# A QKV projection on one core: the first load of x issued as two transfers of one row tile each

## The chip, the cores and the metric

The kernel runs on one core of a Trainium2 chip. Its engines run their own instruction streams side by side: TensorE (PE; its weight loads are listed as PEld), VectorE (DVE), ScalarE (ACT), GpSimd (POOL) and SyncE (SP), which here only issues DMA transfers. Sixteen DMA engines move the bytes. The metric is the device time of one execution in microseconds (us); lower is better.

## The reference

x has 16 x 512 rows of 768 numbers, 8192 rows in all, and w_qkv is 768 x 2304. One product gives q, k and v, which are stacked:

```python
def reference(x, w_qkv):
    qkv = np.matmul(x, w_qkv)
    hidden = x.shape[-1]
    q = qkv[..., :hidden]
    k = qkv[..., hidden:2*hidden]
    v = qkv[..., 2*hidden:]
    return np.stack([q, k, v], axis=0).astype(np.float32)
```

## The kernel before, in words

The 8192 rows are worked on as 32 pairs of row tiles; a row tile has P = 128 rows, and a pair is 256 rows x 768 numbers, 768 KB in fp32. The contraction of K = 768 is cut into KT = 6 slices of 128. Of the 2304 output columns, 2048 are cut into four blocks of 512, which belong to two halves q = 0 and 1, and 256 remain (`rem`). From pair 2 on, a pair and a half q are multiplied by a scheme with seven products in place of eight (`product`, L247), on sums of blocks of x and w that VectorE and GpSimd make ahead. The first two pairs are done by plain bf16 products (`block`, L480), because the sums of w are not there yet.

The order of the work on each engine is the order in which the program writes it (`manual_schedule`, L57). Waits are put in by the tile framework: an instruction waits for whatever wrote the part of a tile that it reads. DMA transfers on SP's queue take eight semaphores in turn, and a transfer is issued only once the transfer eight before it on that rotation has landed.

What happens at the start, in the order in which it is written:

- L452: VectorE clears the tile `zero`.
- L453: `load_rows(0)` loads pair 0 in row order into `xin`, a tile of 128 x 2 x 768: partition m holds row m of both row tiles. It is one transfer of 768 KB (L162).
- L456: `load_rows(1)` does the same for pair 1.
- L457 to L463: the loads of the weights: the first block of 512 columns in six transfers of 256 KB (`load_blocks(0, 0, 1)`), the second in two of 768 KB, the remaining columns (`st_rem`), pair 2 of x in eight pieces (L460, L462), and so on. All go through SP's queue.
- L538: ten matmuls on `zero` on TensorE (`busy(10)`, L469), whose results nobody reads.
- L539: `cast_rows(0)` rounds pair 0 to bf16 row tile by row tile: for each r, VectorE takes the first 384 numbers of each row (L165) and ScalarE the others (L166).
- L540: `turn_rows(0)` transposes pair 0 on TensorE, six transposes for each row tile (L185); VectorE (L194) and ScalarE (L192) copy the results to `xb`. `cast_rows(1)` stands between the two engines' copies.
- L541 to L546: two more matmuls on `zero`, the casts of the first weights' slices (L476), then `turn_rows(1)`, and the casts of the other slices.
- L547: `block(0, 0, ...)`: the first real matmuls (L496), by slices of the weights as these come in: slices 0 and 1 for the two row tiles of pair 0, then the same for pair 1, then slices 2 to 5 for all four row tiles.

From there to the end TensorE has a long stream of matmuls (L258, L321, L496).

Of the kernel before, what the change touches and what calls it, by code (L numbers as in the profile page):

```python
# [10 lines left out]
def kernel(  # L11
# [20 lines left out]
    nc = tc.nc  # L32
    P = 128
# [20 lines left out]
    x_flat = x.rearrange("b t h -> (b t) h")  # L54
# [66 lines left out]
    xin, xf, xb, sr = {}, {}, {}, {}  # L121
# [34 lines left out]

    def load_rows(p):
        xin[p] = xin_pool.tile([P, 2, K], fp32, name="xin")  # L160
        rows = x_flat[p * 2 * P:(p + 1) * 2 * P, :]
        nc.sync.dma_start(xin[p][:], rows.rearrange("(r m) k -> m r k", m=P))  # L162

    def copy_halves(dst, src):
        nc.vector.tensor_copy(out=dst[0], in_=src[0])  # L165
# [284 lines left out]
    ND = 2  # L450
    zero = xb_pool.tile([P, CB], bf16, name="zero", tag="xb")
    nc.vector.memset(zero[:], 0.0)  # L452
    load_rows(0)  # L453
    nc.scalar.activation(tiny[:], zero[:, :1], ident)
    make_identity(nc, eye)
    load_rows(1)  # L456
    load_blocks(0, 0, 1)  # L457
    load_blocks(0, 1)
# [246 lines left out]
```

## Time and profile before

| | |
|---|---|
| median of 3 runs | 359.29 us (359.18 to 359.3) |
| the profiled execution's own time | 358.81 us |
| its span, first to last instruction | 357.0 us |
| TensorE busy | 350.6 us (98%) |
| VectorE, ScalarE, GpSimd busy | 264.4, 185.0, 177.3 us |
| moved by DMA | 108.10 MB, 303 GB/s over the span |
| first load of x issued, and read by the casts | 0.74 us, 4.97 us |
| second load of x issued, and read by the casts | 1.24 us, 6.93 us |
| first matmul of the first block | 8.29 us |

Busy time counts an engine's working instructions. Times in the timeline are microseconds from the first instruction of the span; a matmul's end is modelled, so that the end of one and the start of the next can overlap. In the chain of work that ended last, every link is what the next one waited for.

### The profile page before, as it was taken

Reading aid. Unit: us, or ns where it says so; the run is one execution under the profiler, and the core shown is the slowest. Engines: PE = TensorE matmul, PEld = TensorE weight load, DVE = VectorE, ACT = ScalarE, POOL = GpSimd, SP = SyncE. Lnnn points to the kernel's source line nnn. Section 1 sums busy time; section 2 is a strip of 40 time slices with the busy share of each in tenths; the row PEclk is TensorE's granted clock in tenths of the full one; section 3 lists DMA queues with packets and bytes.
Section 4 is the critical chain, followed back from the end, with each engine's and each line's share of the span. In section 5 each row is a group of like instructions: output and inputs, shape, how many; then the busy total and the mean of one; then the engine's idle time right before and its main releaser. Section 6 shows DMA issues by size and latency. Waiting matters only on the chain.

```text
span 357.0 us, 5315 instructions
## 1 busy us (share of the span) xinstructions
PE 350.6 (98%) x1757; PEld 252.1 (71%) x1776; DVE 264.4 (74%) x310; ACT 185.0 (52%) x317; POOL 177.3 (50%) x184
## 2 busy tenths in 40 slices
PE   7999999999999999999999999999999999999996
PEld 3474677768677686877768677686877768677674
DVE  3789876796877869777695877869777695876743
ACT  4587754545454553645545454553645545454553
POOL 0031773376566453665535566353665535566320
PEclk9999999999999999999999999999999999999999
DMA  7997999999999898998979899698999979887497
GB/s 296 380 353 238 325 378 340 373 317 348 308 311 340 257 361 206 347 266 285 361 197 385 227 342 307 209 402 213 347 263 307 331 196 392 225 303 280 155 380 260
DMA packets 82075, 108.10 MB, mean 303 GB/s; under 512 B 4992, under 2 KB 62080, under 8 KB 82048
## 3 DMA queue, kind: packets, MB, share of 16 engines
q1 hardware_dynamic: 75088, 102.52, 85.7%
q10 hardware_dynamic: 6960, 5.24, 5.5%
q8 instruction: 14, 0.23, 0.3%
q14 instruction: 13, 0.11, 0.1%
HBM read 32.24 MB, written 75.50 MB: 302 GB/s over the span
## 4 chain that ended last, share of the span: by engine, by line
PE 74%; POOL 15%; DVE 6%; issue 3%; DMA 2%; ACT 0%; SPq 0%
PE ps L258 56%; PE ps L321 12%; PE ps L496 6%; DVE xf L155 6%; POOL xb L205 5%; POOL s L226 3%; POOL s L225 3%; POOL s L227 3%; DMA xin<-in_x_dram 2%; PE ps L185 0%; DVE o L304 0%; ACT xc L166 0%; SPq L162 0%; DVE orem L424 0%; ACT orem L423 0%
## 5 line engine op out<-in xcount | busy, mean ns | idle before, releaser
L258 PE MATMUL ps<-t,s 128*128 128x512 f32 x720 | 177.9, 395 | 0.0
L258 PEld LDWEIGHTS ps<-t,s 128*128 128x128 f32 x720 | 135.1, 188 | 29.5
L155 DVE STREAM_TRANSPOSE xf<-xin 128x768 f32<-128x768 f32 (+1 forms) x45 | 93.3, 2075 | 4.3 <-DMA xin<-in_x_dram 4.3
L258 PE MATMUL ps<-b,xb 128*128 128x512 bf16 x343 | 81.6, 379 | 1.1
L298 DVE TENSOR_TENSOR o<-o,ps 128x512 f32<-128x512 f32 x56 | 38.5, 688 | 50.7 <-ACT o L297 50.0
L205 POOL CAST xb<-xf 128x1536 bf16<-128x1536 f32 x28 | 41.1, 1467 | 56.9 <-DVE xf L155 54.8
L225 POOL TENSOR_TENSOR s<-xf 128x384 fp32r<-128x384 f32 x29 | 31.0, 1068 | 72.9 <-DVE xf L155 71.1
L258 PEld LDWEIGHTS <-xb 128*128 128x128 bf16 x360 | 33.9, 98 | 36.7 <-issue 3.9
L304 DVE TENSOR_TENSOR o<-o,ps 128x512 f32<-128x512 f32 x60 | 41.1, 687 | 20.5 <-PE ps L258 19.4
L297 ACT ACTIVATE o<-ps 128x512 f32<-128x512 f32 x56 | 33.5, 598 | 42.1 <-PE ps L258 42.1
L258 PE MATMUL ps<-b,s 128*128 128x512 f32 x180 | 50.6, 389 | 0.0
L301 ACT ACTIVATE o<-ps 128x512 f32<-128x512 f32 x60 | 35.9, 598 | 25.2 <-PE ps L258 22.8
L378 DVE TENSOR_TENSOR o<-o,ps 128x512 f32<-128x512 f32 x78 | 47.8, 680 | 0.0
L321 PE MATMUL ps<-w_rem,xb 128*128 128x256 bf16 x384 | 47.4, 273 | 0.0
L286 ACT ACTIVATE o<-ps 128x512 f32<-128x512 f32 x60 | 35.9, 599 | 19.4 <-PE ps L258 14.0
L321 PEld LDWEIGHTS <-xb 128*128 128x128 bf16 x384 | 37.3, 98 | 11.5 <-issue 0.5
L335 ACT ACTIVATE orem<-ps 128x512 f32<-128x512 f32 x31 | 18.5, 598 | 48.3 <-PE ps L321 34.0
L258 PEld LDWEIGHTS ps<-b,s 128*128 128x128 f32 x180 | 33.8, 188 | 7.0
L226 POOL TENSOR_TENSOR s<-s,xf 128x384 fp32r<-128x384 f32 x29 | 29.5, 1018 | 2.3
L227 POOL TENSOR_TENSOR s<-xf 128x384 fp32r<-128x384 f32 x29 | 29.4, 1015 | 0.0
L229 POOL TENSOR_TENSOR s<-xf,s 128x384 fp32r<-128x384 f32 x29 | 29.2, 1008 | 0.0
L382 ACT ACTIVATE o<-ps 128x512 f32<-128x512 f32 x26 | 15.5, 598 | 17.9 <-PE ps L258 17.3
(49 smaller groups left out, 161.2 us busy)
## 6 DMA issues: line engine op xcount, KB each, us to landing
out_dram<-o SPq DMA_DIRECT2D x60, 768.0 KB, 4.6
out_dram<-o SPq DMA_DIRECT2D x75, 256.0 KB, 3.8
xin<-in_x_dram SPq DMA_DIRECT2D x88, 192.0 KB, 5.6
out_dram<-orem SPq DMA_DIRECT2D x31, 256.0 KB, 2.2
xin<-in_x_dram ACTq DMA_DIRECT2D x24, 192.0 KB, 4.4
st<-in_w_qkv_dram SPq DMA_DIRECT2D x5, 768.0 KB, 7.9
xin<-in_x_dram SPq DMA_DIRECT2D x2, 768.0 KB, 4.9
st<-in_w_qkv_dram SPq DMA_DIRECT2D x6, 256.0 KB, 6.0
```

The lines of the kernel that those rows point to most:

```text
L155: nc.vector.transpose(turned[:, g:g + n], rows[:, g:g + n])
L205: nc.gpsimd.tensor_copy(out=xb[p][:], in_=xf[p][:])
L225: 1: lambda g: g.tensor_tensor(s[:, 1], a21, a22, op=add),
L226: 2: lambda g: g.tensor_tensor(s[:, 2], s[:, 1], a11, op=sub),
L227: 3: lambda g: g.tensor_tensor(s[:, 3], a11, a21, op=sub),
L258: nc.tensor.matmul(ps[:], lhs[j], rhs[j], start=(start and j == 0), stop=(j == KH - 1), skip_group_check=True,)
L286: nc.scalar.activation(c12, u.x[:], ident)
L298: nc.vector.tensor_tensor(c22, c22, u.y[:], op=add)
L301: nc.scalar.activation(c21, u.x[:], ident)
L304: nc.vector.tensor_tensor(c12, c12, u.y[:], op=add)
L321: nc.tensor.matmul(ps, xb[p][:, j, r * P:(r + 1) * P], w_rem[j // KH][:, j % KH, :], start=(j == 0), stop=(j == KT - 1), skip_group_check= ...
L378: dve.tensor_tensor(c, c, u.z[:], op=add)
```

## The change

`load_rows` gets a second argument, a list of parts, each a slice of the partitions and of the row tiles, and issues one transfer per part. Its default is the whole tile as one transfer, so that `load_rows(1)` is what it was. The first call gives two parts: all 128 partitions of row tile 0, then all 128 partitions of row tile 1. In place of one transfer of 128 x 2 x 768 numbers there are two of 128 x 768, one behind the other on SP's queue, into the same tile. Each cast of row tile 0 then waits for the first of them alone, and each cast of row tile 1 for the second. Line numbers below L162 grow by one.

```diff
-    def load_rows(p):
+    def load_rows(p, parts=((slice(0, P), slice(0, 2)), )):
         xin[p] = xin_pool.tile([P, 2, K], fp32, name="xin")
-        rows = x_flat[p * 2 * P:(p + 1) * 2 * P, :]
-        nc.sync.dma_start(xin[p][:], rows.rearrange("(r m) k -> m r k", m=P))
+        rows = x_flat[p * 2 * P:(p + 1) * 2 * P, :].rearrange("(r m) k -> m r k", m=P)
+        for m, r in parts:
+            nc.sync.dma_start(xin[p][m, r], rows[m, r])
...
-    load_rows(0)
+    load_rows(0, [(slice(0, P), r) for r in range(2)])
     nc.scalar.activation(tiny[:], zero[:, :1], ident)
     make_identity(nc, eye)
     load_rows(1)
```

## The prediction

> **What bounds the kernel now.** I read the page's first two parts, then the chain that ended last at the start of the kernel, then the timeline of that stretch, then the DMA rate in half-microsecond windows. The page first: engine totals and the share of the chain by engine.
>
> ```profile
> PE 350.6 (98%) x1757; PEld 252.1 (71%) x1776; DVE 264.4 (74%) x310; ACT 185.0 (52%) x317; POOL 177.3 (50%) x184
> ...
> PE 74%; POOL 15%; DVE 6%; issue 3%; DMA 2%; ACT 0%; SPq 0%
> ```
>
> TensorE works 350.6 of 357.0 us. The change touches only the first load, so it can move the end only if it moves when TensorE's unbroken stream begins. The chain (start, length, what) says what sets that:
>
> ```profile
> 0.74 0.44 SPq L162
> 1.18 0.06 issue
> 1.24 5.67 DMA xin<-in_x_dram
> 6.91 0.02 issue
> 6.93 0.53 ACT xc L166
> ...
> 7.51 0.95 PE ps L185 x12
> 8.46 2.82 PE ps L496 x13
> ...
> 11.33 7.50 PE ps L496 x34
> ```
>
> The link that ends last is the second load of x (issued at 1.24, landed at 6.91), not the first. Behind it come ScalarE's cast of pair 1, its transposes and, from 8.46, matmuls without a gap worth naming. The timeline of the same stretch (start, length, engine, line, operation, idle before):
>
> ```profile
> 0.74 0.95 SPq L162 DMA_DIRECT2D xin<-in_x_dram  x2
> ...
> 1.19 4.30 PE L469 MATMUL ps<-zero 128*128 128x512 bf16 x10 [1.19 <-DVE zero L452]
> ...
> 4.97 0.94 ACT L166 ACTIVATE xc<-xin 128x384 bf16<-128x384 f32 x2 [2.74 <-DMA xin<-in_x_dram]
> 4.97 0.63 DVE L165 CAST xc<-xin 128x384 bf16<-128x384 f32 x2 [3.84 <-DMA xin<-in_x_dram]
> ...
> 6.12 0.77 DVE L194 COPY xb<-ps 128x384 bf16<-128x384 bf16 x2 [0.52 <-PE ps L185]
> ...
> 6.93 0.94 ACT L166 ACTIVATE xc<-xin 128x384 bf16<-128x384 f32 x2 [1.02 <-DMA xin<-in_x_dram]
> ...
> 7.51 0.95 PE L185 MATMUL ps<-eye,xc 128*128 128x128 bf16 x12 [0.58 <-ACT xc L166]
> ...
> 8.26 0.43 DVE L476 CAST b<-st 128x512 bf16<-128x512 f32 x1 [0.27 <-DMA st<-in_w_qkv_dram]
> ...
> 10.85 0.43 DVE L476 CAST b<-st 128x512 bf16<-128x512 f32 x1 [0.28 <-DMA st<-in_w_qkv_dram]
> ```
>
> The casts of pair 0 wait for the first load until 4.97. TensorE is in its ten filler matmuls until 5.49 all the same, and it later stands still for 0.58 us because pair 1 is late. The windows (stretch, busy time of the engines, clock, DMA share, GB/s):
>
> ```profile
> 1.50:2.00 0.50, 0.50 (x2) 0.15 (x1) 0.00 (x0) 0.50 (x1) 0.00 (x0) 1.00 0.57 86
> 2.00:2.50 0.50, 0.50 (x3) 0.21 (x2) 0.00 (x0) 0.22 (x2) 0.00 (x0) 1.00 0.46 92
> 2.50:3.00 0.50, 0.50 (x3) 0.23 (x2) 0.00 (x0) 0.00 (x0) 0.00 (x0) 1.00 0.80 264
> 3.00:3.50 0.50, 0.50 (x3) 0.17 (x2) 0.00 (x0) 0.00 (x0) 0.00 (x0) 1.00 1.01 412
> ```
>
> The transfers start slowly and from 3.0 us run at some 410 GB/s. So the landing at 6.91 is bytes at full rate behind a slow start.
>
> **The change, part by part.** Nothing is removed from the work: the same 768 KB go to the same tile, as two transfers of 384 KB in place of one.
>
> *The rows land apart.* Load 0 is usable at 4.97 and load 1, of the same size, at 6.93: 1.96 us for 768 KB when queued, 0.98 for half. So row 0 should be usable near 4.97 - 0.98 = 3.99, and row 1 at 4.97 as before. Row 0's casts (ScalarE 0.47, VectorE 0.32 us) move from 4.97 to 3.99; row 1's start at 4.97 in place of 5.3 to 5.4. ScalarE then ends pair 0 near 5.50 in place of 5.91.
>
> *What that is worth to TensorE.* The transposes of pair 0 stand behind the ten fillers (1.19 + 4.30 = 5.49) and began at 5.55: 0.06 us to gain. The twelve took 0.95 us with a wait for ScalarE's second cast among them, so perhaps 0.2 us more. Both are given back at once: next in TensorE's order are two fillers and then pair 1's transposes, which need load 1's landing. The idle 0.58 us grows to about 0.8. On the path: 0. Next late is load 1, as now. VectorE, which ended its copies at 6.89 and so was free only just before 6.93, gets some 0.2 us of air; it gains nothing either.
>
> *One more issue on SP.* The two issues of L162 take 0.95 us, some 0.5 each, so everything behind is issued 0.5 us later: load 1 at 1.75 in place of 1.24, the six pieces of the weights' first block each 0.5 later. What hides it: the DMA engines have load 0's bytes to move until nearly 4.97, three microseconds past the later issue, and the pieces find load 1's 1.96 us ahead of them. Were that cover gone, the cost would be the 0.5 us, 359.8.
>
> *One wait more.* Transfers on SP's queue take turns on eight semaphores, and each waits for the one eight before. With one more at the head, the sixth piece of the weights becomes the ninth transfer and waits for row 0's landing; before, it waited for nothing. That wait ends near 4.0, and the piece could not be issued before 4.37 (its issue in SP's own rows) + 0.5 = 4.87 anyway: nothing. Behind it stands the first three-slice load of the second block; it waits for row 1 at 4.97 as it waited for load 0 at 4.97, is issued some 0.4 us later, and has over 4 us of queued bytes in front. All transfers after that wait for the same predecessors as before, and no instruction of TensorE or GpSimd changes.
>
> *The cost of a transfer of its own.* The trace has no split load. Bounds come from the nearest rows: VectorE's waits for pieces at 8.26 and 10.85 are four pieces of 256 KB apart, 0.65 us each or 405 GB/s; the 768 KB load took 1.96, or 401 GB/s. Three small pieces cost as much as one large transfer (1.94 against 1.96), so a queued transfer's own cost is 0 within some 0.03 us. That is the lower end. The upper end is the very first load: 0.74 to 4.97 is 4.23 us, 2.27 above the 1.96. I take 0.02, since row 1 is queued like the pieces and not first in an empty queue. A gain is not excluded: the slow start costs (412 GB/s x 1.16 us - 221 KB) / 412 = 0.62 us by the windows from the first bytes near 1.84 to 3.0, and a shorter first transfer might start otherwise.
>
> The Trainium skill, page "DMA: Bandwidth & Descriptors", section "Rules for kernel authors", speaks against the change: it wants 1 MiB or more per transfer for full bandwidth and small ones merged. The trace does not bear it out between 256 and 768 KB (405 against 401 GB/s), which is why the rival below built on it is small.
>
> The sum: load 1 lands 0.02 us later and all of TensorE's stream with it. The profiled execution has span 357.0 and 1.81 us around it, 358.81; with 0.02 it is 358.83. The median of the runs, 359.29, is 0.48 above that execution, so I put 0.02 on the median: 359.31, in round numbers 359.3.
>
> **The rivals.**
> - *The head of the queue runs better.* The slow start shrinks, and load 1 and the pieces land sooner. For it: 0.62 us lies there, and VectorE is now free in time to use it. Against: total bytes and issue time of the first transfer stay. TensorE's own order bounds it: 0.58 idle + 0.06 + 0.2 = 0.84 us, 358.45.
> - *The slow start comes again at row 1.* Price 0.62 us, at most the whole 1.16 us of 1.84 to 3.0: 359.9 to 360.45. For it: each engine's first packets were slow. Against: load 1, queued too, moved at full rate from its start (412 GB/s in the window from 3.0, 406 in that from 4.0 to 5.0).
> - *A transfer's fixed cost is paid by each.* This is the other side: row 1 or load 1 starts only when what is before it has landed. Price 2.27 us, 361.6; it decides from 0.72 us, a third of it. Against: the row at 6.93 came 1.96 us after that at 4.97, with no such cost. The skill's page named above has a fixed cost of some 2.0 us in its fit for the GpSimd path (section "Anatomy of one DMA — SWDGE (gpsimd) path"); by that the time would be 361.3.
> - *TensorE's clock falls in the longer gap.* The fillers ran at 0.43 us each until about 5 us, later matmuls at 0.217 (2.82 / 13). Were the 0.8 us idle enough to lose the full rate, another 4 us at half would cost some 2 us: 361.3. Against: the 0.58 us gap now did not lose it, as the 0.217 after it shows.
> - *The change doesn't do what it says*: the casts wait for both transfers. Then row 0's casts stay at 4.97 and the time is the forecast's, since nothing follows from them.
>
> **How the numbers follow.** About 0.2% (0.72 us) is what a measurement of this kernel can tell from no change. Nothing moves (with or without early casts): 0.50, 359.0 to 359.6. Better head: 0.20, of which 0.11 beyond 0.2%, where it fills the whole gap. Slow start again: 0.14, half of it beyond. Fixed cost: 0.08. Clock: 0.05. Other causes: 0.03, two thirds of it faster. So faster 0.13, slower 0.07 + 0.08 + 0.05 + 0.01 = 0.21, same 0.66. The range takes in the better head and the slow start but for its last tenth or so, and leaves out the fixed cost and the clock: 358.4 to 360.3.
>
> **What would show it.** Right: in the timeline of the changed kernel VectorE's and ScalarE's first casts stand alone near 4.0 and the second ones at 4.97; pair 0's transposes start near 5.5; pair 1's casts stay at 6.93, the idle before its transposes is near 0.8, and L496 follows at 8.46. The prediction is wrong if the casts of pair 1 move by more than 0.3 us, if TensorE's matmuls after the gap run at 0.43, or if L496 begins later though pair 1's casts do not, which would be the weights' pieces (their 0.5 us later issue) showing.

## The result, and the profile after

The change makes the kernel slower: 361.54 us median (360.51 to 363.76) against 359.26 (359.09 to 359.4), a ratio of 1.0073 with a 95% interval of 1.0048 to 1.0097. The forecast was 359.3, the range 358.4 to 360.3. The profiled execution took 360.70 us with a span of 358.9, 1.9 us more than before's 357.0. The kernel before repeats itself to 0.3 us; the changed one is spread over 3 us, and the profiled execution is one of its fastest, 0.84 us below the median.

First the two lines of the changed kernel's page that answer to those of before: engine totals, and the chain that ended last by engine.

```profile
PE 351.7 (98%) x1776; PEld 252.2 (70%) x1776; DVE 264.1 (74%) x310; ACT 185.4 (52%) x317; POOL 177.3 (49%) x184
...
PE 93%; DMA 4%; SPq 1%; DVE 1%; ACT 0%; issue 0%; DVEq 0%
```

TensorE works as long as before, within what missing records allow; 1.9 us have come in as waiting. The timeline of the changed kernel's start (start, length, engine, line, operation, idle before) shows where:

```profile
3.60 0.52 ACT L167 ACTIVATE xc<-xin 128x384 bf16<-128x384 f32 x1 [1.37 <-DMA xin<-in_x_dram]
...
5.62 0.52 ACT L167 ACTIVATE xc<-xin 128x384 bf16<-128x384 f32 x1 [1.50 <-DMA xin<-in_x_dram]
...
8.16 0.94 ACT L167 ACTIVATE xc<-xin 128x384 bf16<-128x384 f32 x2 [2.02 <-DMA xin<-in_x_dram]
8.74 0.95 PE L186 MATMUL ps<-eye,xc 128*128 128x128 bf16 x12 [1.57 <-ACT xc L167]
...
9.53 5.34 PE L497 MATMUL ps<-b,xb 128*128 128x512 bf16 x24
...
19.23 0.56 DVE L560 CAST w_rem<-str 128x768 bf16<-128x768 f32 x1 [0.83 <-DMA str<-in_w_qkv_dram]
...
20.61 3.04 DVE L155 STREAM_TRANSPOSE xf<-xin 128x768 f32<-128x768 f32 x2 [0.82 <-DMA xin<-in_x_dram]
...
23.13 1.47 PE L259 MATMUL ps<-b,xb 128*128 128x512 bf16 x6
...
24.44 1.47 PE L322 MATMUL ps<-w_rem,xb 128*128 128x256 bf16 x12
```

Row 0 is read 1.37 us earlier than the whole load was (3.60 against 4.97). But load 1, which nothing in the change touches, is read at 8.16 in place of 6.93, TensorE stands idle 1.57 us in place of 0.58, and the first block starts at 9.53 in place of 8.29: +1.24. The other 0.6 us have come in by 24.44, the answer to before's 22.58 (+1.86): the remaining columns of w are cast at 19.23 in place of 17.28, and VectorE's transposes of pair 2 start at 20.61 in place of 18.62, because these loads are late too. The same places in the kernel before:

```profile
17.28 0.56 DVE L559 CAST w_rem<-str 128x768 bf16<-128x768 f32 x1
...
18.62 3.17 DVE L155 STREAM_TRANSPOSE xf<-xin 128x768 f32<-128x768 f32 x2 [0.78 <-DMA xin<-in_x_dram]
...
22.58 1.47 PE L321 MATMUL ps<-w_rem,xb 128*128 128x256 bf16 x12
```

The chain of the changed kernel (start, length, what) goes through that wait, no longer through load 1:

```profile
2.64 6.82 DMA st<-in_w_qkv_dram
...
9.48 0.66 SPq L92
...
10.18 1.77 SPq L137
...
12.64 7.86 DMA xin<-in_x_dram
...
20.61 1.60 DVE xf L155
...
22.23 0.85 ACT xb L215
...
23.13 1.47 PE ps L259 x6
```

It shows transfers waiting for landings and pair 2's x behind them. The windows of the changed kernel (stretch, busy times, clock, DMA share, GB/s) show what the DMA engines do while load 1 should arrive:

```profile
2.00:2.50 0.50, 0.50 (x3) 0.21 (x2) 0.00 (x0) 0.22 (x2) 0.00 (x0) 1.00 1.03 399
...
3.50:4.00 0.50, 0.50 (x2) 0.15 (x1) 0.36 (x1) 0.41 (x1) 0.00 (x0) 1.00 0.92 295
4.00:5.00 1.00, 1.00 (x5) 0.40 (x4) 0.00 (x0) 0.12 (x1) 0.00 (x0) 1.00 0.90 203
5.00:5.50 0.50, 0.47 (x7) 0.33 (x5) 0.00 (x0) 0.00 (x0) 0.00 (x0) 1.00 0.78 264
```

The start is better than before's in this trace (399 GB/s at 2.0 to 2.5, before 92). The loss comes after it: 203 GB/s at a busy share of 0.90, so the engines are counted busy with few bytes. The packet records say the same: in the kernel before no packet of 3072 bytes takes over 256 ns between 2.75 and 6 us; in the changed kernel some take up to 1025 ns between 4 and 5 us. A load is there when the last of the sixteen DMA engines has reported: in the kernel before the last report on load 1 comes at 6.91, and the cast reads it at 6.93. The reports on load 1, in us, with some kernels of the next section:

```
                                      first   middle   last engine
before                                 6.36    6.71     6.91
changed                                6.51    6.91     8.14
changed, again                         6.41    6.59     8.50
before, load 1 issued at 1.58          6.29    6.71     8.50
before, load 1 issued at 3.55          7.44    7.70     7.88
changed, pieces of w issued late       6.25    6.55     8.96
before, a small transfer ahead         6.75    7.24     7.53
changed, load 1 on ScalarE's queue     5.52    5.70     6.06
```

In both traces of the changed kernel the middle engine reports at most 0.2 us later than before, or even sooner. The last one is 1.2 and 1.9 us behind the middle one, and it sets the time. (With the issue at 3.55, and with the small transfer ahead, it is otherwise: there all engines report late, and close together.)

### The profile page after: what moved, and what is told of

Same layout as the page of the kernel before. It is cut to its first block, busy times and chain, and to the rows that moved or that the text cites. A ratio compares the mean times of both kernels' runs of the same rounds, so it can differ in the third digit from the quotient of the medians.

```text
span 358.9 us, 5335 instructions
## 1 busy us (share of the span) xinstructions
PE 351.7 (98%) x1776; PEld 252.2 (70%) x1776; DVE 264.1 (74%) x310; ACT 185.4 (52%) x317; POOL 177.3 (49%) x184
## 4 chain that ended last, share of the span: by engine, by line
PE 93%; DMA 4%; SPq 1%; DVE 1%; ACT 0%; issue 0%; DVEq 0%
PE ps L259 79%; PE ps L322 11%; PE ps L497 3%; DMA xin<-in_x_dram 2%; DMA st<-in_w_qkv_dram 2%; SPq L137 1%; DVE xf L155 0%; SPq L163 0%; SPq L92 0%; ACT xb L215 0%; DVE orem L425 0%; ACT orem L424 0%; DVEq L155 0%
## 5 line engine op out<-in xcount | busy, mean ns | idle before, releaser
L259 PE MATMUL ps<-b,xb 128*128 128x512 bf16 x360 | 85.4, 380 | 0.1
```

The source lines that it names most:

```text
L259: nc.tensor.matmul(ps[:], lhs[j], rhs[j], start=(start and j == 0), stop=(j == KH - 1), skip_group_check=True,)
```

## The experiments

Times are medians; a ratio is to the kernel before, run on the same chip in turn, with its 95% interval. Each run has one trace. The granted clock is the share of its full speed that TensorE was given. "Load 1 read" is the first cast of pair 1, at 6.93 in the kernel before. Line numbers differ a little between kernels.

**The changed kernel again.** No edit.

> The changed kernel itself once more. What its first trace shows: row 0 is usable early (3.60 us), row 1 at 5.62 and the second load at 8.16 us, because the DMA engines stand still or have single packets of up to 1 us just behind the end of row 0 and of row 1. If this lies in the kernel and not in that one execution, the second load is again usable later than 7.5 us (before: 6.93) and the time is 360.3 to 363.8. If it was chance, the second load is usable near 6.95 in this trace.

362.14 us, ratio 1.0085 (1.0070 to 1.0100). Load 1 read at 8.52, rows at 3.88 and 4.82. So the late load 1 belongs to the kernel. Row 1's delay in the first trace (5.62) does not come again; here it is read 0.94 us behind row 0.

**More fillers in the gap.**

```diff
-    busy(2)
+    busy(8)
```

> The changed kernel with eight matmuls on zeros ahead of pair 1's transposes in place of two (six more, 0.22 us each, 1.3 us in a gap that was 1.57 us in the changed kernel's trace). Theory of the clock (of the 1.2 to 4.5 us lost, what varies from run to run is a falling TensorE clock in the longer gap): the granted clock is 1.000 in every run and the times lie within 0.5 us of each other, near 360.0 to 360.8. If the spread comes from the DMA alone, it stays (over 1.5 us between runs) and the median stays near 361.5.

361.86 us, ratio 1.0084 (1.0067 to 1.0101); granted clocks 0.998 to 1.000, against 0.995 to 0.999 without the fillers. Load 1 is read at 8.51, the same as in the trace before it (8.52), so the two can be set side by side. First the changed kernel again: one row of its timeline and two of its windows.

```profile
9.10 1.25 PE L186 MATMUL ps<-eye,xc 128*128 128x128 bf16 x12 [2.12 <-ACT xc L167]
...
10.00:11.00 1.00, 1.00 (x6) 0.45 (x4) 1.00 (x4) 0.67 (x3) 0.00 (x0) 0.50 1.06 395
11.00:12.00 1.00, 1.00 (x4) 0.44 (x3) 0.76 (x3) 0.42 (x2) 0.00 (x0) 0.50 1.02 393
```

Then the kernel with more fillers:

```profile
9.09 0.95 PE L186 MATMUL ps<-eye,xc 128*128 128x128 bf16 x12 [0.84 <-ACT xc L167]
...
10.00:11.00 1.00, 1.00 (x7) 0.43 (x5) 1.00 (x4) 0.66 (x3) 0.00 (x0) 1.00 1.05 395
11.00:12.00 1.00, 1.00 (x6) 0.45 (x5) 0.79 (x3) 0.41 (x2) 0.00 (x0) 1.00 1.05 406
```

After 2.12 us of idle the granted clock is 0.50, after 0.84 it is 1.00; the spans are 360.2 and 359.3, so the fallen clock cost some 0.9 us in this pair of traces. It is a part of the loss in some executions and not its main part: with the fillers the time is still 361.08 to 362.09, and their other three executions, at clocks of 0.998 to 1.000, have spans of 360.0 to 360.3, as long as the trace with the fallen clock. Nor do the fillers narrow the spread: it is 1.0 us with them and 1.0 us in the four executions without them that were measured beside them, where the theory of the clock gave 0.5.

**The first load cut by partitions.**

```diff
-    load_rows(0, [(slice(0, P), r) for r in range(2)])
+    load_rows(0, [(slice(m, m + P // 2), slice(0, 2)) for m in (0, P // 2)])
```

> The first load in two transfers by partitions (64 partitions, both rows, 384 KB each) in place of rows. Theory of the queue (a second short transfer at the head of an empty queue makes the engines run dry at each boundary): the second load is usable near 8 us and the time is 360.3 to 363 as in the changed kernel, though the casts of pair 0 start only when both halves are there. Theory of the addresses (it is the sixteen engines' walk through one row tile of x that the memory serves slowly, and every engine here alternates between the row tiles as before): the second load is usable near 6.95, the time 359.0 to 359.6.

362.77 us, ratio 1.0105 (1.0071 to 1.0140); load 1 read at 9.18, pair 0 only at 6.86. Its windows:

```profile
3.50:4.00 0.50, 0.50 (x3) 0.15 (x1) 0.00 (x0) 0.00 (x0) 0.00 (x0) 1.00 1.22 240
4.00:4.50 0.50, 0.50 (x2) 0.15 (x1) 0.00 (x0) 0.00 (x0) 0.00 (x0) 1.00 0.91 203
```

Here most packets between 3.5 and 5.5 us take 200 to 260 ns, the middle one 231 in place of 121: these transfers to 64 partitions run at about half the rate. That is another effect, and it hides the one sought, so this run decides nothing.

**The second load cut by rows, the first whole.**

```diff
-    load_rows(0, [(slice(0, P), r) for r in range(2)])
+    load_rows(0)
...
-    load_rows(1)
+    load_rows(1, [(slice(0, P), r) for r in range(2)])
```

> The first load whole, the second load of x in two transfers by rows. Theory of the queue: the first load's 768 KB cover the time until the descriptors behind are ready, so row 1 of pair 1 is usable within 0.3 us of 6.93 and the time is 359.0 to 359.8. Theory of the addresses: the rows of pair 1 are slow in the same way, their second one usable at 7.5 or later, the time 359.9 or more.

359.56 us, ratio 1.0014 (1.0004 to 1.0023). The second row of pair 1 is there at 7.09 and read at 7.12. The cut costs some 0.5 us when it stands second, about a fifth of what it costs at the head, as the theory of the queue said; the addresses of single row tiles are not to blame.

**No early casts.**

```diff
-        for r in range(2):
+        for r in ((1, 0) if p == 0 else (0, 1)):
             halves = (slice(0, K // 2), slice(K // 2, K))
```

> The changed kernel with pair 0's casts in the other order, row 1 before row 0: the transfers are the same, but no cast runs before row 1 is there (about 4.8 us in place of 3.6 to 3.9). Theory of the casts (casts that run while SP is still issuing the weights' pieces hold up the making of descriptors; SP's issues of 1.2 to 1.3 us at 3.6 to 4.1 us stand beside the early casts): no issue over 0.7 us before 4.8 us, the second load usable by 7.3, the time 359.0 to 360.0. Theory of the queue (short transfers at the head of the queue, or the early landing of row 0 itself): nothing changes, the long issue and a second load after 8 us stay, the time is 361 to 362.5.

361.46 us, ratio 1.0058 (1.0039 to 1.0077). The first cast runs at 4.78, yet load 1 is read at 7.88, and an issue on SP is long again (1.01 us from 3.64; in the kernel before none of the first eight takes over 0.63). The theory of the casts falls. The next two put casts where there were none before.

**Idle casts in the kernel before**, on VectorE, and five on ScalarE at 2.13 to 4.85 us in the other kernel:

```diff
+    nc.vector.memset(both[:, 0, :K // 2], 0.0)
+    for _ in range(9):
+        nc.vector.tensor_copy(out=both[:, 1, :K // 4].bitcast(bf16), in_=both[:, 0, :K // 2])
```

> The kernel before with nine more casts of 128 x 384 on VectorE (0.36 us each) on a tile that nobody has loaded yet, from about 1.3 to 4.5 us, while SP issues. Transfers as before. Theory of the casts, on VectorE: issues over 1 us appear on SP, the second load is usable at 7.5 us or later, the time rises by 0.7 us or more. Theory of the queue: the second load stays within 0.2 us of 6.93 and the time within 0.4 us of the kernel before.

> The kernel before with five more casts of 128 x 384 on ScalarE (0.47 us each) from about 2.3 to 4.7 us. Theory of the casts, on ScalarE: the second load at 7.5 us or later and 0.7 us or more on the time. Theory of the queue: the second load within 0.2 us of 6.93 and the time within 0.4 us of the kernel before.

359.40 us, ratio 1.0000 (0.9991 to 1.0010), and 359.29 us, 1.0001 (0.9991 to 1.0010). Both traces read load 1 at 6.86. The one with VectorE's casts:

```profile
1.57 3.52 DVE L456 CAST both<-both 128x384 bf16<-128x384 f32 x9
...
6.86 0.94 ACT L166 ACTIVATE xc<-xin 128x384 bf16<-128x384 f32 x2 [0.90 <-DMA xin<-in_x_dram]
```

Casts beside the transfers cost nothing here. That settles the casts.

**A small transfer ahead of everything in the kernel before.**

```diff
+    nc.sync.dma_start(both[:, 0, :P], x_flat[:P, :P])
     load_rows(0)
```

> The kernel before with one small transfer (128 x 128 numbers of x, 64 KB, 512 bytes a partition, to a tile loaded later) ahead of the first load: it lands near 2.6 us while SP is still issuing, no cast reads it, and everything behind is issued one place later, as in the changed kernel. Theory of the queue: a short transfer at the head makes the engines run dry at its end, a long issue appears on SP, the second load is usable at 7.5 us or later, and the time rises by 0.7 us or more. Theory of the casts: the second load is usable at 7.1 to 7.4 (6.93, 0.15 us of bytes and a later start), and the time is 359.0 to 359.6.

359.91 us, ratio 1.0021 (1.0010 to 1.0032); load 1 read at 7.55. It lies between the two theories: 0.62 us late, and one issue of 0.92 us on SP. The timeline shows where the 0.62 us come from:

```profile
5.62 0.94 ACT L166 ACTIVATE xc<-xin 128x384 bf16<-128x384 f32 x2 [3.39 <-DMA xin<-in_x_dram]
...
7.55 0.94 ACT L166 ACTIVATE xc<-xin 128x384 bf16<-128x384 f32 x2 [1.00 <-DMA xin<-in_x_dram]
```

Load 0 is read 0.65 us late already (5.62 against 4.97). It is issued 0.45 us later, at 1.19, and has some 0.16 us of added bytes ahead (64 KB at 410 GB/s). Load 1 follows it by 1.93 us, as in the kernel before (1.96), and no engine is far behind the others (0.78 us from the first to the last). So load 1, third in the queue and issued at 1.66 as in the changed kernel, is not held up here.

**Fewer requests on SP while load 1 comes.** First, the pieces of the weights from the third on held back until 4.7 us: the third waits for a small clear, which VectorE does behind eight idle casts:

```diff
+            if nj == 1:
+                nc.vector.memset(t[:, 2, :1], 0.0)
             for j in range(0, KT, nj):
...
+    nc.vector.memset(both[:, 0, :K // 2], 0.0)
+    for _ in range(8):
+        nc.vector.tensor_copy(out=both[:, 1, :K // 4].bitcast(bf16), in_=both[:, 0, :K // 2])
```

> The changed kernel, but the weights' pieces from the third on are issued only from about 4.7 us on (they wait for a one-column clear that VectorE does after eight idle casts), so SP issues nothing between about 3.1 and 4.7 us; the pieces issued late have two loads and two pieces of bytes ahead of them. Theory of crowding (the engines stall at the ends of the short transfers because SP's requests for the pieces are being worked on just then): no issue over 0.7 us, the second load is usable by 7.4 us, the time is 359.0 to 360.2. Theory of dry engines (an engine that runs out at the end of row 0 or row 1 loses time by itself, whatever is issued later): the second load stays at 7.8 us or later and the time at 360.5 or more.

363.02 us, ratio 1.0110 (1.0089 to 1.0131). SP issues nothing between 3.1 and 4.7 us and no issue is longer than 0.69, yet load 1 is read at 8.98:

```profile
8.98 0.94 ACT L169 ACTIVATE xc<-xin 128x384 bf16<-128x384 f32 x2 [3.75 <-DMA xin<-in_x_dram]
```

Second, the first block in two transfers in place of six:

```diff
-    load_blocks(0, 0, 1)
+    load_blocks(0, 0)
```

> The changed kernel with the first block of weights in two transfers of 768 KB in place of six of 256 KB: after the three loads of x SP has fewer requests to work on. Its first slices of the weights come later by construction (a slice is there only with the two others of its transfer, about 1.3 us), so the landing of the second load is what counts, not the time. Theory of crowding, by the number of requests: the second load is usable by 7.4 us. Theory of dry engines: 7.8 us or later.

364.10 us, ratio 1.0137 (1.0120 to 1.0154); load 1 read at 9.04. The theory of crowding falls: SP's later requests do not make load 1 late. Nor does a long issue on SP: the first of these two kernels has none before 4.7 us and stalls all the same.

**The first load cut by columns**, in halves, and at 640 of 768 (`load_rows` takes a third slice, of the columns; in the uneven kernel the two are 0 to 640 and 640 to 768):

```diff
+    load_rows(0, [(slice(0, P), slice(0, 2), slice(n, n + K // 2)) for n in (0, K // 2)])
```

> The first load in two transfers by columns: 384 of the 768 numbers of every row of both row tiles, 384 KB each, over all 128 partitions, in pieces of 1536 bytes. Every engine goes over the same rows in the same order as in the kernel before. Theory of the addresses: the second load is usable by 7.2 us. Theory of the queue (a first transfer of only half the bytes): a long issue on SP, the second load at 7.8 us or later, 360.3 us or more.

> As the one before, but uneven: first 640 of the 768 numbers of every row (640 KB, 1.6 us at full rate), then the other 128 (128 KB). Theory of the queue, by the bytes of the first transfer: with five sixths of the first load's bytes ahead the descriptors behind are ready in time, the second load is usable by 7.3 us, the time 359.0 to 360.0. If it is the number of transfers at the head and not the bytes of the first: 7.8 us or later and 360.3 us or more, as with the halves.

361.63 us, ratio 1.0073 (1.0049 to 1.0098), load 1 read at 9.27; and 362.00 us, 1.0080 (1.0065 to 1.0095), load 1 read at 8.73. Neither the order of addresses nor the bytes of the first transfer matters: five sixths of them ahead do not help. What these kernels share with the change is that load 1 is the third transfer and is issued near 1.7 us, but so it is with the small transfer ahead, where it is not held up.

**Only the issue of load 1 moved, no transfer added.** Load 1 waits for a small clear of its tile, behind a clear and 0, 1, 3 or 5 idle casts on VectorE; what SP issues behind load 1 moves with it:

```diff
+    nc.vector.memset(both[:, 0, :K // 2], 0.0)
+    for _ in range(1):  # 0, 1, 3, 5
+        nc.vector.tensor_copy(out=both[:, 1, :K // 4].bitcast(bf16), in_=both[:, 0, :K // 2])
...
         xin[p] = xin_pool.tile([P, 2, K], fp32, name="xin")
+        if p == 1:
+            nc.vector.memset(xin[p][:, :, :1], 0.0)
```

> The kernel before with the second load issued near 1.6 us (a clear of VectorE's ahead of it), close to the 1.66 us of the changed kernel, and no transfer added. Theory of the issue time: the second load is usable at 7.5 to 8.5 us and the time is 360.0 to 362.0, as in the changed kernel. Theory of the transfer added at the head: 6.9 to 7.2 us and 358.9 to 359.7.

> The kernel before with the second load issued near 2.1 us in place of 1.24 (it waits for a small clear of its tile by VectorE); no transfer is added. Theory of the late descriptors, in the form that descriptors are made one transfer after the other at about 5 ns each from 1.84 us on (first load ready near 2.7 to 3.1, second near 4.4, needed from 4.1): a small loss, the second load usable at 6.9 to 7.4 us, the time 358.9 to 359.8. Theory of a fixed delay from the issue of a transfer to its packets of some 2.6 us: needed at 4.1, ready at 4.7, the second load at 7.5 us or later. Theory of the transfer's end: no change, 6.93.

> The same with the issue near 2.8 us. By a delay that grows with the issue time (ready a fixed time after it) the landing would lie between or above those of 1.97 and 3.55 us, 8.0 to 8.5 us. If the loss belongs to a stretch of the start (some 1.6 to 2.4 us), the second load is usable at 6.9 to 7.5 us, since 2.8 + 1.1 = 3.9 us is still before the engines need it.

> As the one before, but the second load is issued near 3.6 us, so that its first packets can hardly come before 4.7 us (1.1 us after the issue, as with the first load) while the engines end the first load between 4.1 and 4.6. By the missing bytes alone the second load would be usable at 7.1 to 7.5 us. If an engine that runs out of descriptors loses more than the gap itself, as in the changed kernel, it is usable at 8 us or later and the time is 360.3 or more. Theory of the transfer's end (a short transfer ends early): no stall beyond the gap, 7.1 to 7.5 us and 359.0 to 360.0.

The issue of load 1 and the first cast that reads it, in the timelines. With no idle cast:

```profile
1.58 0.37 SPq L164 DMA_DIRECT2D xin<-in_x_dram  x1
...
8.52 0.94 ACT L168 ACTIVATE xc<-xin 128x384 bf16<-128x384 f32 x2 [2.58 <-DMA xin<-in_x_dram]
```

With one:

```profile
1.97 0.37 SPq L164 DMA_DIRECT2D xin<-in_x_dram  x1
...
8.43 0.94 ACT L168 ACTIVATE xc<-xin 128x384 bf16<-128x384 f32 x2 [2.36 <-DMA xin<-in_x_dram]
```

With three:

```profile
2.76 0.37 SPq L164 DMA_DIRECT2D xin<-in_x_dram  x1
...
7.91 0.94 ACT L168 ACTIVATE xc<-xin 128x384 bf16<-128x384 f32 x2 [2.01 <-DMA xin<-in_x_dram]
```

With five:

```profile
3.55 0.37 SPq L164 DMA_DIRECT2D xin<-in_x_dram  x1
...
7.90 0.94 ACT L168 ACTIVATE xc<-xin 128x384 bf16<-128x384 f32 x2 [1.86 <-DMA xin<-in_x_dram]
```

The times are 361.69 us (ratio 1.0060, 1.0042 to 1.0079), 361.41 (1.0061, 1.0046 to 1.0076), 361.53 (1.0067, 1.0051 to 1.0083) and 360.53 (1.0041, 1.0025 to 1.0056). The delay by itself is enough: 0.34 us on the issue of load 1 (1.58 in place of 1.24), with the first load in one piece, makes it 1.6 us late and the kernel as slow as the change does. It isn't a fixed delay from issue to packets: issued 2.3 us later than in the kernel before, load 1 is only 1.0 us late, less than when it is issued 0.3 us later. Nor is it descriptors (one for each contiguous piece of a transfer) made one after the other at a steady pace, which gave 6.9 to 7.4 us for the issue at 1.97. The stretch that I had supposed, 1.6 to 2.4 us, is wrong as well: the issue at 2.76 is late too. The kinds of lateness differ, though. With the issue at 1.58 fifteen engines have reported by 6.83 and one comes at 8.50. With the issue at 3.55 all sixteen report between 7.44 and 7.88: here the engines run dry, with 49 GB/s from 5.0 to 5.5 us and 338 in the half microsecond after it, some 2 us behind the issue.

**Half the descriptors for load 1** (each partition takes two neighbouring rows of x in one piece; pair 1's rows of the result are in another order for it):

```diff
-        rows = x_flat[p * 2 * P:(p + 1) * 2 * P, :].rearrange("(r m) k -> m r k", m=P)
+        rows = x_flat[p * 2 * P:(p + 1) * 2 * P, :].rearrange("(r m) k -> m r k" if p == 0 else "(m r) k -> m r k", m=P)
```

> The changed kernel with the second load reading neighbouring rows of x into each partition, so that each partition takes one piece of 6144 bytes in place of two of 3072 (128 descriptors in place of 256); the rows of pair 1's result are in another order for that, which costs no time. Theory of the late descriptors: they are ready near 3.7 us, before the engines need them at 3.9 to 4.2, so the second load is usable by 7.3 us and the time is 359.0 to 360.2. Theory of the transfer's end: 7.8 us or later and 360.5 or more.

362.02 us, ratio 1.0074 (1.0057 to 1.0091); load 1 read at 8.82. The number of its descriptors is not the cause.

**Load 1 on ScalarE's queue, from the start.**

```diff
-            nc.sync.dma_start(xin[p][m, r], rows[m, r])
+            (nc.sync if p == 0 else nc.scalar).dma_start(xin[p][m, r], rows[m, r])
...
+    load_rows(1)
     nc.scalar.activation(tiny[:], zero[:, :1], ident)
     make_identity(nc, eye)
-    load_rows(1)
```

> The changed kernel with the second load issued from ScalarE's hardware queue at about 0.74 us, so that its packets share the engines with the rows' from the start. Theory of the late descriptors: with the second load's descriptors made early, no engine runs dry; all three loads are usable by 7.2 us (row 0 and row 1 later than in the changed kernel, as the bytes are shared), the time is 359.0 to 360.2. Theory of the transfer's end: engines still stall behind row 0 and row 1, the last of the three is usable at 7.8 us or later.

361.12 us, ratio 1.0049 (1.0032 to 1.0067). The timeline (ACTq is ScalarE's queue):

```profile
0.73 0.46 ACTq L163 DMA_DIRECT2D xin<-in_x_dram  x1
0.74 0.87 SPq L163 DMA_DIRECT2D xin<-in_x_dram  x2
...
4.52 0.53 ACT L167 ACTIVATE xc<-xin 128x384 bf16<-128x384 f32 x1 [1.80 <-DMA xin<-in_x_dram]
...
6.92 1.35 ACT L167 ACTIVATE xc<-xin 128x384 bf16<-128x384 f32 x3 [1.88 <-DMA xin<-in_x_dram]
```

All three issues are over by 1.61 us, load 1 is there at 6.06 (table above), and the last of the three is read at 6.92, as in the kernel before. The same two row transfers stand at the head, and the stall is gone: the landings are as the theory of the late descriptors said. The time is not, because row 1, which TensorE takes before pair 1, is now the last to come: TensorE waits 1.86 us for it, and three of the four executions have a granted clock of 0.995. Load 1 is both earlier and on another queue here; this run does not tell the two apart.

**What is shown and what stays open.** That a later issue of load 1 is enough to cause the loss is shown by the kernels before with load 1 held back: no transfer is added or cut there, and the time is the changed kernel's. They add one thing that the change does not have, a wait of SP for VectorE, and no run has that wait without the delay; the changed kernel stalls without it.

The time of the issue alone does not tell a late load 1 from one in time: 1.66 is late in the changed kernel and in time with the small transfer ahead. One figure does, read off the traces afterwards: the lead, from the issue of load 1 (or of its last part) to the report of the middle engine on the transfer ahead of it. The lead is 3.4 to 3.7 us in the kernel before, with the idle casts and with the small transfer ahead, where load 1 is not held up, and 4.0 with the second load cut by rows, where its last engine is 0.3 us behind the next to last. It is 1.2 to 3.2 us wherever load 1 came 1.0 to 2.3 us late: 3.2 with the issue at 1.58, and 2.6 and 3.0 in the two traces of the changed kernel. (ScalarE's queue, where load 1 has no transfer ahead of it, and the cut by partitions, with its slow packets, are left out.) The change shortens the lead at both ends: load 1 is issued 0.42 us later, and the middle engine is done with the row transfers 0.2 to 0.5 us sooner than with the whole load (4.66 and 4.30 against 4.84).

So a request needed a lead of over 3.2 us at this start to reach all engines in time; that is a regularity of these traces, and no run was made to test it. What holds the late engines up (their descriptors or their data) no view shows, and it stays open. No kernel tried beats the kernel before; the nearest were the two with idle casts, at no difference.

## Why the prediction was wrong

- **Where it failed**: "One more issue on SP". The prediction saw that load 1 would be issued later (at 1.75; it was 1.66) and priced that at nothing, because load 0's bytes would keep the engines busy until nearly 4.97, "three microseconds past the later issue". That cover did not hold. The delay alone, put into the kernel before, gives 361.69 us, against 361.54 for the change. Even the price without cover, 0.5 us, was too small: load 1 was 1.24 to 1.6 us late, and the time rose by 2.3 us. The step took the lead of an issue over its bytes as safe without a row that shows how long a request takes to reach all sixteen engines.
- **The cost of a transfer of its own**, 0.02 us, was sized from transfers deep in a full queue. With the cut as the second load the time rose by 0.14%, some 0.5 us: more than the 0.02, though part of it can be the weights, which are issued later there too, and small beside the 2.3 us of the cut at the head.
- **The rivals**: "the slow start comes again at row 1" (0.62 to 1.16 us) had at its upper end nearly what load 1 lost in the first trace (1.24), but half of what the time lost, and for another reason and in another place: the stall is in load 1, and it is there with no second row transfer. (Its argument against, 412 GB/s in the window from 3.0, was of load 0's bytes: load 0 is reported from 4.45 on.) "A transfer's fixed cost is paid by each" had the time, 361.6, by luck, with the wrong mechanism: row 1 came 0.9 to 1.35 us after row 0 in the later traces of the row cut, against 0.98 at full rate, and no 2.27 us after it. "The clock falls" was given 0.05; it fell to a mean of 0.995 or less in four of the eight executions. Its argument (the 0.58 us gap did not lose the rate) said nothing of the 1.57 to 2.1 us that the gap became; the two came together, the longer gap by the late load and in some executions a fallen clock behind the gap.
- **Right**: the rows land apart (row 0 at 3.60 and 3.88 against 3.99 forecast; row 1 at 4.82 in the second trace, 4.97 forecast); early casts are worth nothing to TensorE, since its own order and load 1 come next (the kernel without them, 361.46, is no slower); load 1's landing sets the start of the stream one for one (8.16 - 6.93 = 1.23, 9.53 - 8.29 = 1.24). That last point is what made a late load 1 cost so much.
- **Left out**: the second loss of 0.6 us, at the remaining columns and pair 2's pieces. The prediction rightly had these transfers wait for the same predecessors as before, and put nothing on it; but they are issued only as those land, and the weights' pieces behind load 1 landed late with it (in the chain, 9.46 and the issue at 9.48).

## What to carry to other kernels

Before anything is put ahead of the load that the chain runs through, ask how much later that load will be issued and how much sooner the engines will be through with what stands ahead of it, and hold only a run as proof that the queue hides it: here 0.34 us on one issue at the start cost over 2 us at the end (361.69 against 359.16). Cutting a transfer so that its first half can be used early is worth something only if someone on the critical chain uses it; otherwise cut, if at all, behind the load that is waited for. When a load at the start of a kernel comes late, look also at TensorE's clock in the windows behind the longer gap.

## What the runs showed that I had not expected

- Some DMA engines, with the issue at 1.58 a single one, report 1.2 to 2.4 us behind the middle one on a load with a short lead, while the middle one is nearly on time (table above).
- A later issue can land earlier: load 1 issued at 3.55 was read at 7.90, issued at 1.58 at 8.52 (one trace each; the medians are 360.53 and 361.69).
- Transfers to 64 partitions ran at 203 to 252 GB/s from 3.5 to 5.5 us, about half the rate of 128 partitions (406 to 436 in the kernel before at 3.5 to 5.5). The Trainium skill, page "DMA: Bandwidth & Descriptors", section "Rules for kernel authors", advises against transfers to partition halves because they serialize; the trace agrees with the advice and shows a lower rate besides.
- 2.12 us of idle on TensorE stood ahead of a fall of the granted clock to 0.50, for about 3.4 us (the windows from 9 to 13 us have 0.71, 0.50, 0.50 and 0.58). The length of the idle time alone does not decide it: with the issue at 3.55, 1.42 us of idle were followed by a fall (0.80 from 8 to 9 us, 0.50 from 9 to 12), and with the cut at 640 columns 2.19 us were not (1.00 from 7 to 12). The Trainium skill, page "TensorE: Matmul & The Clock Gate", section "Part 1: The HAM clock gate", has a window of 3.4 us and says that an idle window of that length brings the half clock. The length at half clock agrees; unbroken idle time of that length was not needed here.
